# The later modulation vectors of layer 0: two pairs of column blocks gathered in one accumulator bank

## The chip, the cores and the metric

The kernel runs on one core of a Trainium2 chip. The metric is the device time of one execution in microseconds (us); the median of three runs of the kernel before is 1124.67 us.

## What is computed

A two-layer backbone on 512 tokens of width 1024 with a context prefix of 256 tokens. Everything is float32. What matters here is the modulation: six vectors of 1024 values for each layer, made from one conditioning vector c.

```python
def ada_mod(cvec, w, b, dtype):
    m = jax.nn.silu(cvec.astype(jnp.float32)) @ w.astype(jnp.float32) + b.astype(jnp.float32)
    return jnp.split(m.astype(dtype), N_MOD, axis=-1)
...
sh1, sc1, g1, sh2, sc2, g2 = ada_mod(c, w_ada[i], b_ada[i], h.dtype)
n_x = modulate(rms_norm(h, norm_mix_g[i]), sh1, sc1)
...
y_x, _, _ = even_mixer(n_x, ep, s_f, s_b)
h = h + g1[:, None] * y_x
h = h + g2[:, None] * sq_relu_mlp(modulate(rms_norm(h, norm_mlp_g[i]), sh2, sc2), mlp_w1[i], mlp_w2[i])
```

The even mixer of layer 0 joins a bidirectional state-space scan over 32 channel groups with a gated convolution, and ends in an output projection. The change touches the third to fifth vector of layer 0 (g1, sh2, sc2), which are needed only from the output projection on.

## The kernel before, in words

The program is a list of tile operations in `mixer0` and in the stage behind it. A scheduler decides in which order each engine gets them, so a small edit can move many instructions. Each engine runs its own queue strictly in order: TensorE (PE, with its weight loads PEld), VectorE (DVE), ScalarE (ACT), GpSimd (POOL) and the one DMA queue, which SyncE (SP) issues.

**Where the change sits.** In `mixer0` the input projection comes first, then eight steps of the scan (`step_params` prepares a step, `step_main` runs it: `ps_v` on PE, the chain `rr`, `tv`, scan, `ua`, `ub` on DVE, copies `sc` on ACT, `ps_y` on PE). Other work is filled in between the steps by a table of letters: `FILL0` behind the first three `step_params`, `FILL` behind the steps. `v` is a projection of the convolution branch (`ps_vg`, 48 matmuls), `c` a convolution (`ps_cv`), `y` and `z` the outputs of the scan (`ps_t`, `ge`), `k` and `g` the gate (`gw`, `ps_gl`), `h` the load of the residual stream, `n` the norm of the convolution (`ps_mu`, `ps_ms`, `ps_r`), `w` the output projection (`ps_o`), and `a3` means three calls of `ada_rest`.

**The later modulation vectors.** `ada_rest(m, d)` makes 2 x 128 columns of vector m. The 1024 conditioning values lie in `S2` as eight slices of 128 rows, each padded with zeros to 32 columns, so that a slice can be the stationary operand of a quarter of the array. `ada_pe` (L353 to L370) loads two blocks of 128 columns (512 KB each, L223), and for each block issues eight matmuls of 128 columns, four of them side by side in the four column groups (L363). The four partial sums lie in four groups of 32 partitions of the bank `ps_ada`; ACT copies them to `ada` (L139), and one small matmul for each block (L369) with the selector `sel` adds the four and turns the row into a column. DVE adds the bias into `mod` (L113). There are 12 such calls: 24 loads, 192 tile matmuls, 24 small ones, 12 copies and 12 additions. Float32 matmuls leave two records each in the trace.

**What they share.** The loads go through the ring `wraw` of three buffers, which also holds the projection weights (`win_vg`), the weights of the last convolution (`CW`), those of the gate (`wglu`) and of the output projection (`wout`). A load is issued when the buffer's user three allocations earlier is done, and whatever stands behind it on the DMA queue waits too: the shifted copies for the convolution (`cvt<-vpad`), the small transfers of the scan's kernels (`Kt<-sd`, and `hx<-sd` for steps 2 and 5), and the residual stream. `ps_ada` shares a pair of banks (tag "c") with `ps_vg`, `ps_cv` and others.

```python
for i, w in enumerate(ws):
    for kt in (0, 2, 4, 6, 1, 3, 5, 7):
        j = kt // 2
        PE.matmul(ps[32 * j:32 * j + 32, i * 128:i * 128 + 128], S2[:, kt, :], w[kt],
                  start=kt % 2 == 0, stop=kt % 2 == 1, tile_position=(0, 32 * j))
```

Of the kernel before, what the change touches and what calls it, by code (L numbers as in the profile page):

```python
# [8 lines left out]
F32 = mybir.dt.float32  # L9
# [10 lines left out]
KT = 8  # L20
# [25 lines left out]
    g="VVVVVVVVVVVVVVVVVVVVVVVVVVVVVVVVVVVVVVVVVVVVVVVV", e="VVVVVVVVVVVVVVVVVVVVVVVVVVVVVVVVVVVVVVVVVVVVVVVV", o="VVVVVVVVVVVVVVVVVVVVVVVVVVVVVVVVVVVVVVVVVVVVVVVV",  # L46
    ra="VVVVVVVVVVVVVVVV", um="VVVVVVVVVVVVVVVVVVVVVVVVVVVVVVVV", ua="VVVVVVVVVVVVVVVVVVVVVVVVVVVVVVVV",
    wv="VVVVVVVV", ln="VVVV", wo="VVVVVVVVVVVVVVVV",
    w="VVVVVVVV", wdb="VVVVVVVV", wub="VVVVVVVV",
# [5 lines left out]
WT = "cc"  # L55
YB = 1
AT = "c"
WU = "r"
REV = (1,)
CWH = ("h", "h", "h", "wraw")  # L60
# [7 lines left out]
XQ = "P"  # L68
OQ = "P"
FOG = 2  # L70
FILL0 = ("v0 a3", "", "")
FILL = ("v1", "", "c0 v2 a2", "c1 c2 v3", "a3 y", "c3", "h k a4 n", "w7 z", "g w9 w9")
NREST = (1, 1, 1, 1, 2, 2, 2, 2)
NB = 16
LB = 5
# [22 lines left out]
def body(tc, I, out, dbg=None):  # L98
    nc = tc.nc
    V, S, G, PE = nc.vector, nc.scalar, nc.gpsimd, nc.tensor  # L100
# [8 lines left out]
    def mul(e, o, a, b):  # L109
        e.tensor_tensor(o, a, b, op=OP.mult)  # L110

    def add(e, o, a, b):
        e.tensor_tensor(o, a, b, op=OP.add)  # L113
# [23 lines left out]
    def copy(e, o, a):  # L137
        if e is S:
            S.activation(o, a, AF.Copy)  # L139
        else:  # L140
            e.tensor_copy(o, a)
# [10 lines left out]
    with tc.tile_pool(name="persist", bufs=1) as P, tc.tile_pool(name="ps", bufs=1, space=PSUM) as PS:  # L152
# [5 lines left out]
        mod = P.tile([128, 2, 6, KT], F32, name="mod")  # L158

        def smv(n):  # L160
            o, w = SM[n]
            return sm[:, o:o + w]

        bada = smv("bada").rearrange("p (l m) -> p l m", l=2)
# [35 lines left out]
        def bank(nm, tag):  # L200
            return PS.tile([128, 512], F32, name=nm, tag=tag, bufs=dict(s=2, c=2, m=1, n=1)[tag])
# [103 lines left out]
        def mixer0(P0):  # L305
            ring = Ring(P0, RING0)
# [9 lines left out]
            sd = P0.tile([128, GQ, 15 * PH], F32, name="sd")  # L316
            stage = sd[0:PH]
            Dd = sd[32:32 + PH].rearrange("p a b -> p (a b)")[:, 0:NG * PH].rearrange("p (q h) -> p q h", h=PH)
            S2 = P0.tile([128, KT, 32], F32, name="S2")
            sel = P0.tile([128, 32], F32, name="sel")  # L320

            def w4(nm, tag, dt=F32, n=512):
# [13 lines left out]

            G.memset(S2, 0.0)
            cs = P0.tile([128, 2, KT], F32, name="cs")
            cT = smv("c").rearrange("p (v k) -> p v k", v=2)
            S.activation(cs, cT, AF.Sigmoid)  # L340
            mul(V, S2[:, :, 0:2].rearrange("p k v -> p v k"), cT, cs)
            V.tensor_reduce(sel, ident.rearrange("p (j r) -> p r j", j=4), axis=mybir.AxisListType.X, op=OP.add)

            def ada_half(src):
# [9 lines left out]
            def ada_pe(srcs, ld, tag="n"):  # L354
                n = len(srcs)
                ws = [l(src) for l, src in zip(ld, srcs)]

                def go():
                    ps = bank("ps_ada", tag)
                    for i, w in enumerate(ws):  # L360
                        for kt in (0, 2, 4, 6, 1, 3, 5, 7):
                            j = kt // 2
                            PE.matmul(ps[32 * j:32 * j + 32, i * 128:i * 128 + 128], S2[:, kt, :], w[kt],  # L363
                                      start=kt % 2 == 0, stop=kt % 2 == 1, tile_position=(0, 32 * j))
                    a = P0.tile([128, 256], F32, name="ada", tag="ada", bufs=1)[:, :n * 128]
                    copy(S, a, ps[:, 0:n * 128])
                    p2 = ps[:, 256:256 + 2 * n]
                    for i in range(n):
                        PE.matmul(p2[:, 2 * i:2 * i + 2], a[:, i * 128:i * 128 + 128], sel[:, 0:2], start=True, stop=True)  # L369
                    return p2.rearrange("p (m v) -> p m v", v=2)  # L370
                return go
# [45 lines left out]
            def u_load(d):  # L417
                adas[d] = ada_pe([I["wada0"][d, 0], I["wada0"][d, 1]], (ada_half, ada_full))
                wus[d] = w4("wu", WU[d % len(WU)])
                dma(wus[d], I["win_u"][d])  # L420
# [77 lines left out]
            dt_, a2, ea, em = small(), small(2 * NG), small(2 * NG), small(2 * NG)  # L498
# [402 lines left out]
            for i in range(0, NG, 4):  # L901
                ps = bank("ps_u", UT[i // 4])
# [14 lines left out]
            x4 = cvt[:, 0:4 * X4].rearrange("p (c t) -> p c t", c=4)  # L917
            cw = smv("cw").rearrange("p (j x) -> p j x", j=4)

            def ada_rest(m, d):  # L920
                p2 = ada_pe([I["wada0b"][m - 2, d], I["wada0b"][m - 2, d + 1]], (ada_full, ada_full), AT)()
                add(V, mod[:, 0, m, d:d + 2], p2[:, :, 0], bada[:, 0, m * KT + d:m * KT + d + 2])

            rest = [(m, d) for m in (2, 3, 4) for d in range(0, KT, 2)]
            ysbs = []
            cacc = []
            vps = []
# [3 lines left out]
            def fill(what):  # L931
                for x in what.split():
                    if x[0] == "v":
                        vps.append(vgt(int(x[1])))
                    elif x == "z":
                        y_out(1, ysbs[1])
                    elif x == "y":
                        y_out(0, ysbs[0])
                    elif x == "k":
                        glu_load()  # L940
                    elif x == "g":
                        glu_gate()
                    elif x == "n":
                        conv_norm(cacc)
                    elif x == "h":
                        hh.append(htile("h", [128, KT, L]))
                        load_x(hh[0], "xT")
                        for d in range(KT):
                            add_pos(E("hp", d), hh[0], d)
                    elif x[0] == "w":  # L950
                        for _ in range(int(x[1])):
                            p, t, d = oparts.pop(0)
                            out_proj(ring, hh[0], d, (p,), HALF[t], WT)
                    elif x[0] == "c":
                        cacc.append(conv(int(x[1]), vps[int(x[1])]))
                    else:
                        for _ in range(int(x[1])):
                            ada_rest(*rest.pop(0))

            for st in range(3):  # L960
                QS.append(step_params(st))
                fill(FILL0[st])
            for st in range(NST):
# [3 lines left out]
                if st + 3 < NST:  # L967
                    QS.append(step_params(st + 3))
                fill(FILL[st])
            fill(FILL[NST])  # L970
            ts(mod[:, 0, 4], mod[:, 0, 4], 1.0, OP.add)
# [3 lines left out]
        with tc.tile_pool(name="pre", bufs=1) as P0:  # L975
            EPOS = (V, G, V, G, V, G, V, G)
            h, oparts = mixer0(P0)


        with tc.tile_pool(name="main", bufs=1, reuse_waits="tile") as M:  # L980
            crow = M.tile([128, D], F32, name="crow", tag="junk")
            csil = M.tile([128, D], F32, name="csil", tag="csil")
            ring = Ring(M, RING1)


            for t, tk in enumerate(HALF):
                for d in range(KT):
                    ps = tuple(p for p in (1, 0) if (p, t, d) in oparts)
# [87 lines left out]
            for i in range(2):  # L1076
                w = ring.raw(I["pw"][2 * i:2 * i + 2].rearrange("g p m k c -> p g m k c"), [2, 2, 2, 128])
# [67 lines left out]
            for tk in HALF:  # L1145
                n = tk.stop - tk.start
# [43 lines left out]
def layout(inp):  # L1190
    a = {k: np.asarray(v) for k, v in inp.items()}
    X = {}
# [20 lines left out]
    X["sm"] = np.concatenate([parts[n] for n in SM], axis=1)  # L1213
    wa = a["w_ada"].reshape(2, KT, 128, 6, KT, 128)
    X["wada0"] = wa[0][:, :, 0:2].transpose(3, 2, 1, 0, 4)
    X["wada0b"] = wa[0][:, :, 2:5].transpose(2, 3, 1, 0, 4)
    wt = a["w_ada"].transpose(0, 2, 1)
    X["wadaT"] = np.concatenate([wt[0, 5 * D:].reshape(KT, 128, D), wt[1].reshape(6 * KT, 128, D)], axis=0)
    perm = [(2 * bb + gh) * 8 + i for bb in range(2) for i in range(8) for gh in range(2)]
# [49 lines left out]
```

## Time and profile before

| | |
|---|---|
| median of three runs (range) | 1124.67 us (1123.05 to 1126.91) |
| the profiled execution, and its span | 1127.26 us, 1125.1 us |
| PE busy | 1045.0 us, 93% of the span |
| DVE busy | 810.7 us, 72% |
| ACT busy | 514.6 us, 46% |
| mean granted TensorE clock | 0.969 of full |

The profiled execution took 2.2 us more than its span, and 2.6 us more than the median of the runs. Shares over the whole span are averages: the mixer fills the first third, where PE, DVE and the DMA queue wait for each other in turn; the MLPs fill the rest, where PE is nearly always busy. What an edit in the mixer is worth is read from the stretch in which it sits. In the rows below a timeline row gives the start, the time from the first start to the last end of what it merges, the engine, the line and the operation, and in brackets the idle time before it and what ended that. "Granted clock" (PEclk) is TensorE's clock as a share of 2.4 GHz.

### The profile page before, as it was taken

Reading aid. Unit: us, or ns where it says so; the run is one execution under the profiler, and the core shown is the slowest. Engines: PE = TensorE matmul, PEld = TensorE weight load, DVE = VectorE, ACT = ScalarE, POOL = GpSimd, SP = SyncE. Lnnn points to the kernel's source line nnn. Section 1 sums busy time; section 2 is a strip of 40 time slices with the busy share of each in tenths; the row PEclk is TensorE's granted clock in tenths of the full one; section 3 lists DMA queues with packets and bytes.
Section 4 is the critical chain, followed back from the end, with each engine's and each line's share of the span. In section 5 each row is a group of like instructions: output and inputs, shape, how many; then the busy total and the mean of one; then the engine's idle time right before and its main releaser. Section 6 shows DMA issues by size and latency. Waiting matters only on the chain.

```text
span 1125.1 us, 18913 instructions
## 1 busy us (share of the span) xinstructions
PE 1045.0 (93%) x7342; PEld 892.9 (79%) x7342; DVE 810.7 (72%) x1511; ACT 514.6 (46%) x910; POOL 23.8 (2%) x44
## 2 busy tenths in 40 slices
PE   3879998985998999999999999989989999999996
PEld 2657665544788988888789999989989988888896
DVE  7965699778688989868746679899866553343365
ACT  4365544454755643313325456566545332133253
POOL 0002000000000000000000000000000000000000
PEclk9999899997899999999999999999989999999998
DMA  9430634145546788878745555545535522233252
GB/s 348 146 128 30 184 85 148 44 123 187 160 137 208 208 281 290 304 230 282 242 149 170 182 174 186 162 133 177 160 121 181 178 94 94 95 108 97 94 169 94
DMA packets 63594, 185.09 MB, mean 165 GB/s; under 512 B 8464, under 2 KB 14608, under 8 KB 63376
## 3 DMA queue, kind: packets, MB, share of 16 engines
q1 hardware_dynamic: 63504, 183.87, 50.6%
q8 instruction: 58, 0.95, 0.3%
q14 instruction: 32, 0.26, 0.1%
HBM read 175.22 MB, written 2.10 MB: 158 GB/s over the span
## 4 chain that ended last, share of the span: by engine, by line
PE 53%; DMA 8%; DVE 6%; ACT 1%; issue 1%; POOLq 0%; POOL 0%; DVEq 0%; ACTq 0%
PE ps L150 17%; PE ps L149 17%; PE ps L148 17%; DMA wraw<-in_wadaT 5%; DMA wraw<-in_w 3%; DVE junk L1000 2%; DVE wlo L116 2%; ACT whi L139 1%; PE ps_o L148 0%; PE ps_r L194 0%; DVE tn L125 0%; PE ps_o L150 0%; PE ps_o L149 0%; PE ps_p L150 0%; PE ps_p L148 0%
## 5 line engine op out<-in xcount | busy, mean ns | idle before, releaser
L139 ACT ACTIVATE whi<-wraw 128x1024 fp32r<-128x1024 f32 (+1 forms) x232 | 231.7, 1000 | 397.2 <-PE ps L149 268.9
L116 DVE TENSOR_TENSOR wlo<-wraw,whi 128x1024 fp32r<-128x1024 f32 (+1 forms) x232 | 266.3, 1149 | 107.4 <-ACT whi L139 104.5
L148 PE MATMUL ps<-nh,whi 128*128 128x256 f32 (+3 forms) x768 | 245.8, 322 | 4.4 <-ACT nh L285 2.5
L150 PE MATMUL ps<-nh,wlo 128*128 128x256 f32 (+3 forms) x768 | 246.4, 322 | 1.8 <-DVE wlo L116 1.7
L149 PE MATMUL ps<-nl,whi 128*128 128x256 f32 (+3 forms) x768 | 246.7, 322 | 1.2 <-DVE nl L125 1.2
L148 PE MATMUL ps<-hh,whi 128*128 128x512 f32 (+3 forms) x768 | 244.3, 318 | 0.0
L150 PE MATMUL ps<-hh,wlo 128*128 128x512 f32 (+3 forms) x768 | 243.7, 317 | 0.1
L149 PE MATMUL ps<-hl,whi 128*128 128x512 f32 (+3 forms) x768 | 243.4, 317 | 0.0
L148 PEld LDWEIGHTS ps<-nh,whi 128*128 128x128 f32 x768 | 148.0, 194 | 15.7 <-ACT nh L285 3.7
L150 PEld LDWEIGHTS ps<-nh,wlo 128*128 128x128 f32 x768 | 148.0, 193 | 13.2 <-DVE wlo L116 3.1
L149 PEld LDWEIGHTS ps<-nl,whi 128*128 128x128 f32 x768 | 148.1, 193 | 11.8 <-DVE nl L125 1.7
L150 PEld LDWEIGHTS ps<-hh,wlo 128*128 128x128 f32 x768 | 144.2, 188 | 12.0 <-DVE wlo L116 0.9
L149 PEld LDWEIGHTS ps<-hl,whi 128*128 128x128 f32 x768 | 144.3, 188 | 10.6
L148 PEld LDWEIGHTS ps<-hh,whi 128*128 128x128 f32 x768 | 144.5, 188 | 9.9
L125 DVE SCALAR_TENSOR_TENSOR h<-ps,mod,h 128x512 f32<-128x512 f32 (+3 forms) x96 | 54.9, 571 | 85.9 <-PE ps L150 85.9
L1000 DVE SCALAR_TENSOR_TENSOR junk<-wraw,csil 128x1024 f32<-128x1024 f32 x56 | 68.3, 1220 | 19.9 <-DMA wraw<-in_wadaT 19.6
L116 DVE TENSOR_TENSOR hl<-rl,hh 128x256 fp32r<-128x256 f32 (+3 forms) x96 | 48.5, 511 | 4.8 <-ACT hh L139 3.7
L1026 ACT ACTIVATE rl<-ps 128x256 f32<-128x256 f32 (+3 forms) x96 | 41.9, 437 | 5.7 <-PE ps L150 4.6
L148 PE MATMUL ps_o<-nh,whi 128*128 128x256 f32 x128 | 38.2, 299 | 3.6 <-ACT whi L139 3.0
L150 PE MATMUL ps_o<-nh,wlo 128*128 128x256 f32 x128 | 37.2, 295 | 1.8 <-DVE wlo L116 1.8
L149 PE MATMUL ps_o<-nl,whi 128*128 128x256 f32 x128 | 36.8, 288 | 0.1
L363 PE MATMUL ps_ada<-wraw,S 128*32 128x128 f32 x512 | 25.7, 311 | 9.4 <-DMA wraw<-in_wada0b 8.5
(266 smaller groups left out, 1371.1 us busy)
## 6 DMA issues: line engine op xcount, KB each, us to landing
wraw<-in_w SPq DMA_DIRECT2D x192, 512.0 KB, 3.5
wraw<-in_wadaT SPq DMA_DIRECT2D x56, 512.0 KB, 4.6
wraw<-in_wada0b SPq DMA_DIRECT2D x24, 512.0 KB, 4.4
wraw<-in_wout SPq DMA_DIRECT2D x32, 256.0 KB, 2.6
cvt<-vpad SPq DMA_DIRECT2D x64, 67.5 KB, 2.0
wah<-in_wada SPq DMA_DIRECT2D x16, 256.0 KB, 3.8
wraw<-in_wada SPq DMA_DIRECT2D x8, 512.0 KB, 8.1
wraw<-in_win_vg SPq DMA_DIRECT2D x8, 512.0 KB, 4.2
```

Source lines behind the costliest of these rows:

```text
L116: e.tensor_tensor(o, a, b, op=OP.subtract)
L125: V.scalar_tensor_tensor(o, a, s, b, op0=op0, op1=op1)
L139: S.activation(o, a, AF.Copy)
L148: PE.matmul(ps, wh, xh, start=first, stop=False)
L149: PE.matmul(ps, wh, xl, start=False, stop=False)
L150: PE.matmul(ps, wl, xh, start=False, stop=last)
L363: PE.matmul(ps[32 * j:32 * j + 32, i * 128:i * 128 + 128], S2[:, kt, :], w[kt], start=kt % 2 == 0, stop=kt % 2 == 1, tile_position=(0, 32 ...
L1000: V.scalar_tensor_tensor(junk, w, 1.0, csil, op0=OP.mult, op1=OP.mult, accum_out=r)
L1026: S.activation(t, ps, AF.Relu)
```

## The change

Two pairs of column blocks now share one bank and one pass. A call of `ada_rest(m, d0)` makes 4 x 128 columns: four loads of 512 KB, each with 4 of the 8 slices and 256 columns (the array on the host is laid out anew for that), and 16 matmuls of 256 columns. For the second pair the stationary slice starts two columns earlier in `S2`, which has eight columns of zeros in front, so that its sums land two partitions further down in the same bank, and all 16 add into it. Then one copy, two small matmuls with the selector columns 0 and 2, and one addition of 4 columns. There are 6 calls in place of 12, and the table of letters places them anew: four pairs behind the first `step_params` (three before), none behind step 2 (two before), four behind step 4 (three before), four behind step 6 (four before).

```diff
-FILL0 = ("v0 a3", "", "")
-FILL = ("v1", "", "c0 v2 a2", "c1 c2 v3", "a3 y", "c3", "h k a4 n", "w7 z", "g w9 w9")
+FILL0 = ("v0 a2", "", "")
+FILL = ("v1", "", "c0 v2", "c1 c2 v3", "a2 y", "c3", "h k a2 n", "w7 z", "g w9 w9")
...
-            S2 = P0.tile([128, KT, 32], F32, name="S2")
+            S2 = P0.tile([128, KT, 40], F32, name="S2")
...
-            def ada_rest(m, d):
-                p2 = ada_pe([I["wada0b"][m - 2, d], I["wada0b"][m - 2, d + 1]], (ada_full, ada_full), AT)()
-                add(V, mod[:, 0, m, d:d + 2], p2[:, :, 0], bada[:, 0, m * KT + d:m * KT + d + 2])
-
-            rest = [(m, d) for m in (2, 3, 4) for d in range(0, KT, 2)]
+            def ada_rest(m, d0):
+                ps = bank("ps_ada", AT)
+                for p in range(NPR):
+                    for kh in range(2):
+                        w = ring.raw(I["wada0b"][m - 2, d0 // 2 + p, kh], [4, 256])
+                        for j in range(4):
+                            PE.matmul(ps[32 * j:32 * j + 32, 0:256], S2[:, 4 * kh + j, 8 - 2 * p:40 - 2 * p], w[:, j],
+                                      start=p == kh == 0, stop=p == NPR - 1 and kh == 1, tile_position=(0, 32 * j))
+                a = P0.tile([128, 256], F32, name="ada", tag="ada", bufs=1)
+                copy(S, a, ps[:, 0:256])
+                p2 = ps[:, 256:256 + 2 * NPR].rearrange("q (i p) -> q i p", i=2)
+                for i in range(2):
+                    PE.matmul(p2[:, i], a[:, i * 128:i * 128 + 128], sel[:, 0:2 * NPR:2], start=True, stop=True)
+                bd, o = (x.rearrange("q (p i) -> q i p", i=2) for x in (
+                    bada[:, 0, m * KT + d0:m * KT + d0 + 2 * NPR], mod[:, 0, m, d0:d0 + 2 * NPR]))
+                add(V, o, p2, bd)
+
+            rest = [(m, d) for m in (2, 3, 4) for d in range(0, KT, 2 * NPR)]
```

The lines of the changed kernel are one higher up to this point. On every engine the order stands as before up to the first of these matmuls, behind the input projection, and again from the output projection on; between them it moves. Three places show how.

On PE, at the start of the scan. `ps_g` turns the first step's operand, `ps_v` is the first step's product (16 matmuls), `ps_vg` the second projection of the convolution branch. Before:

```order
L363 MATMUL ps_ada<-wraw,S_87 32x128 x6
L634 MATMUL ps_g<-ident,gg 128x128 x4
L363 MATMUL ps_ada<-wraw,S_87 32x128 x8
L634 MATMUL ps_g<-ident,gg 128x128 x4
L690 MATMUL ps_v<-U,GT 64x96
L691 MATMUL ps_v<-U,GT 64x96
L690 MATMUL ps_v<-U,GT 64x96
L691 MATMUL ps_v<-U,GT 64x96
L369 MATMUL ps_ada<-sel,ada 128x2 x2
L148 MATMUL ps_vg<-nh,whi 128x512
L149 MATMUL ps_vg<-nl,whi 128x512
L666 MATMUL ps_k<-O,Bb 16x128 x8
```

and in the changed kernel:

```order
L927 MATMUL ps_ada<-wraw,S_87 32x256 x4
L933 MATMUL ps_ada<-sel,ada 128x2 x2
L635 MATMUL ps_g<-ident,gg 128x128 x4
L927 MATMUL ps_ada<-wraw,S_87 32x256 x4
L635 MATMUL ps_g<-ident,gg 128x128 x4
L691 MATMUL ps_v<-U,GT 64x96
L692 MATMUL ps_v<-U,GT 64x96
L691 MATMUL ps_v<-U,GT 64x96
L692 MATMUL ps_v<-U,GT 64x96
L927 MATMUL ps_ada<-wraw,S_87 32x256 x4
L667 MATMUL ps_k<-O,Bb 16x128 x8
L691 MATMUL ps_v<-U,GT 64x96
```

Before, 12 of the 16 `ps_v` stood behind the first two `ps_vg`. Now they stand ahead of them, behind the seventh load's four matmuls; the eighth load's four follow the last `ps_v`.

On PE, in the middle, behind the third projection of the convolution branch. Before:

```order
L363 MATMUL ps_ada<-wraw,S_87 32x128 x2
L634 MATMUL ps_g<-ident,gg 128x128 x4
L363 MATMUL ps_ada<-wraw,S_87 32x128 x8
L666 MATMUL ps_k<-O,Bb 16x128 x8
L363 MATMUL ps_ada<-wraw,S_87 32x128 x6
L690 MATMUL ps_v<-U,GT 64x96
L691 MATMUL ps_v<-U,GT 64x96
L690 MATMUL ps_v<-U,GT 64x96
```

and in the changed kernel, at the end of the same projection:

```order
L151 MATMUL ps_vg<-nh,wlo 128x512
L725 MATMUL ps_y<-Kt,U 64x128 x2
L725 MATMUL ps_y<-O,sc 64x128
L635 MATMUL ps_g<-ident,gg 128x128 x4
L725 MATMUL ps_y<-O,sc 64x128 x3
L725 MATMUL ps_y<-Kt,U 64x128 x2
L725 MATMUL ps_y<-O,sc 64x128 x4
L789 MATMUL ps_cv<-cvt,hx 32x512 x3
L635 MATMUL ps_g<-ident,gg 128x128 x4
L691 MATMUL ps_v<-U,GT 64x96
L692 MATMUL ps_v<-U,GT 64x96
```

The two calls that stood among this step's `ps_g`, `ps_k` and `ps_v` are gone from here; no `ps_ada` stands on PE between the start of the scan and the fourth projection's end.

On the DMA queue, at the fourth to sixth step. `hx<-sd` are the eight transfers for step 5, the first `Kt<-sd` those for step 6. Before:

```order
L780 DMA cvt<-vpad 32x540 x5
L223 DMA wraw<-in_wada0b 128x1024 x2
L678 DMA hx<-sd 16x4x128 x8
L223 DMA wraw<-in_wada0b 128x1024
L780 DMA cvt<-vpad 32x540 x11
L223 DMA wraw<-in_wglu 128x512 x3
L244 DMA h<-in_xT 128x1024
L678 DMA Kt<-sd 16x4x128 x8
L244 DMA h<-in_xT 128x1024 x3
L223 DMA wraw<-in_wglu 128x512
L223 DMA wraw<-in_wada0b 128x1024 x4
L678 DMA Kt<-sd 16x4x128 x8
```

and in the changed kernel:

```order
L224 DMA wraw<-in_wada0b 128x1024 x3
L781 DMA cvt<-vpad 32x540 x5
L224 DMA wraw<-in_wada0b 128x1024 x2
L781 DMA cvt<-vpad 32x540 x9
L224 DMA wraw<-in_wglu 128x512 x2
L679 DMA hx<-sd 16x4x128 x8
L224 DMA wraw<-in_wglu 128x512
L245 DMA h<-in_xT 128x1024 x4
L224 DMA wraw<-in_wglu 128x512
L224 DMA wraw<-in_wada0b 128x1024
L679 DMA Kt<-sd 16x4x128 x8
L224 DMA wraw<-in_wada0b 128x1024 x3
```

Step 5's transfers have moved back, behind five loads of this kind and two of the gate's. Step 6's stood behind one of the four loads of the residual stream and stand now behind all four, a gate load and one more load of this kind.

## Rows read from the trace of the kernel before

**Rows 1.** The page's first part: busy time, share of the span, instructions.
```profile
PE 1045.0 (93%) x7342; PEld 892.9 (79%) x7342; DVE 810.7 (72%) x1511; ACT 514.6 (46%) x910; POOL 23.8 (2%) x44
```

**Rows 2.** Busy us by stretch: PE, PEld, DVE, ACT, POOL; then PEclk, DMA share, GB/s.
```profile
120.00:150.00 30.00, 29.36 (x272) 19.59 (x276) 26.27 (x41) 15.80 (x36) 0.11 (x1) 0.93 0.50 148
150.00:180.00 30.00, 28.27 (x316) 19.60 (x308) 29.49 (x43) 13.09 (x33) 2.23 (x5) 1.00 0.30 73
180.00:210.00 30.00, 27.80 (x216) 17.04 (x207) 27.90 (x47) 15.78 (x39) 0.38 (x4) 0.94 0.46 134
210.00:240.00 30.00, 27.34 (x352) 15.02 (x351) 20.40 (x30) 15.63 (x41) 2.02 (x2) 1.00 0.35 98
240.00:270.00 30.00, 20.43 (x198) 10.55 (x196) 28.32 (x49) 14.33 (x34) 0.11 (x1) 0.89 0.47 152
270.00:300.00 30.00, 25.76 (x231) 19.14 (x232) 20.63 (x41) 19.94 (x38) 1.01 (x1) 0.77 0.52 166
...
400.00:600.00 200.00, 198.77 (x954) 166.39 (x954) 151.69 (x270) 65.97 (x87) 0.00 (x0) 1.00 0.75 247
```

**Rows 3.** Groups of instructions by line, from 100 to 330 us, of `ada_rest`.
```profile
L363 PE MATMUL ps_ada<-wraw,S 128*32 128x128 f32 x384 | 18.6, 311 | 9.3 <-DMA wraw<-in_wada0b 8.5 <-DVE vpad L110 0.7
...
L369 PE MATMUL ps_ada<-sel,ada 128*128 128x2 f32 x48 | 8.1, 274 | 0.6 <-ACT ada L139 0.6
```

**Rows 4.** The tile ps_ada: duration ns min/median/max; first and last start.
```profile
L139 ACT ACTIVATE ada<-ps_ada x20: 361/383/445, 18.1 to 295.1; 128x256 f32<-128x256 f32 x20
L113 DVE TENSOR_TENSOR mod<-ps_ada,sm x12: 138/160/161, 115.2 to 296.6; 128x2 f32<-128x2 f32 x12
```

**Rows 5.** Timeline of PE, full clock: matmuls of 128 columns, 32 wide.
```profile
171.08 0.64 PE L363 MATMUL ps_ada<-wraw,S 128*32 128x128 f32 x16
171.65 0.65 PE L666 MATMUL ps_k<-O,Bb 64*16 64x128 f32 x16
...
175.09 0.42 PE L363 MATMUL ps_ada<-wraw,S 128*32 128x128 f32 x6 [0.70 <-DVE vpad L110]
```

**Rows 6.** Timeline of PE, full clock: the convolution, 512 columns, 32 wide.
```profile
147.27 4.49 PE L788 MATMUL ps_cv<-cvt,hx 128*32 128x512 f32 x38
151.69 0.66 PE L634 MATMUL ps_g<-ident,gg 128*128 128x128 f32 x4
```

**Rows 7.** Timeline of PE at the start of the scan.
```profile
117.34 0.64 PE L363 MATMUL ps_ada<-wraw,S 128*32 128x128 f32 x4 [1.90 <-DMA wraw<-in_wada0b]
...
120.90 1.08 PE L363 MATMUL ps_ada<-wraw,S 128*32 128x128 f32 x16
...
126.78 0.50 PE L150 MATMUL ps_vg<-nh,wlo 128*128 128x512 f32 x1
```

**Rows 8.** Timeline of the DMA queue there (two windows).
```profile
112.13 0.81 SPq L223 DMA_DIRECT2D wraw<-in_wada0b  x2
...
114.57 0.34 SPq L223 DMA_DIRECT2D wraw<-in_win_vg  x1
```

**Rows 9.** Timeline of DVE there: the first step's first product.
```profile
128.27 0.94 DVE L110 TENSOR_TENSOR rr<-ps_v,E 128x768 f32<-128x768 f32 x1
```

**Rows 10.** Timeline of PE from the fourth to the sixth step.
```profile
235.03 0.44 PE L724 MATMUL ps_y<-hx,U 128*64 128x128 f32 x4
...
238.94 0.65 PE L363 MATMUL ps_ada<-wraw,S 128*32 128x128 f32 x16 [1.28 <-DMA wraw<-in_wada0b]
...
262.74 0.70 PE L724 MATMUL ps_y<-Kt,U 128*64 128x128 f32 x4 [6.40 <-DMA Kt<-sd]
```

**Rows 11.** Timeline of the DMA queue there.
```profile
228.48 5.13 SPq L678 DMA_DIRECT2D hx<-sd  x8
...
255.71 0.33 SPq L244 DMA_DIRECT2D h<-in_xT  x1
256.16 5.13 SPq L678 DMA_DIRECT2D Kt<-sd  x8
```

More of the change, by code (lines that the diff above doesn't have):

```diff
@@ L57 @@
 AT = "c"
+NPR = 2
 WU = "r"
@@ L340, in mixer0 @@
             S.activation(cs, cT, AF.Sigmoid)
-            mul(V, S2[:, :, 0:2].rearrange("p k v -> p v k"), cT, cs)
+            mul(V, S2[:, :, 8:10].rearrange("p k v -> p v k"), cT, cs)
             V.tensor_reduce(sel, ident.rearrange("p (j r) -> p r j", j=4), axis=mybir.AxisListType.X, op=OP.add)
@@ L362, in go @@
                             j = kt // 2
-                            PE.matmul(ps[32 * j:32 * j + 32, i * 128:i * 128 + 128], S2[:, kt, :], w[kt],
+                            PE.matmul(ps[32 * j:32 * j + 32, i * 128:i * 128 + 128], S2[:, kt, 8:40], w[kt],
                                       start=kt % 2 == 0, stop=kt % 2 == 1, tile_position=(0, 32 * j))
@@ L957, in fill @@
                         for _ in range(int(x[1])):
-                            ada_rest(*rest.pop(0))
+                            ada_rest(*rest.pop(0)) if rest else None
             for st in range(3):
@@ L1215, in layout @@
     X["wada0"] = wa[0][:, :, 0:2].transpose(3, 2, 1, 0, 4)
-    X["wada0b"] = wa[0][:, :, 2:5].transpose(2, 3, 1, 0, 4)
+    X["wada0b"] = wa[0][:, :, 2:5].reshape(2, 4, 128, 3, 4, 256).transpose(3, 4, 0, 2, 1, 5)
     wt = a["w_ada"].transpose(0, 2, 1)
```

## The prediction

> **What bounds the kernel now.** The busy times come first [rows 1]: PE works 93% of the span, so the question is where it isn't the last to be waited for. The stretches answer that [rows 2]. In the MLP PE is busy 198.77 of 200 us: what the mixer saves is handed on whole, as the order of every engine from the output projection on is unchanged. In the mixer the bound changes hands. From 120 to 210 us both work nearly always (DVE 26.27, 29.49 and 27.90 of 30, PE 29.36, 28.27 and 27.80). From 210 to 240 PE leads (27.34 against 20.40), from 240 to 270 DVE (28.32 against 20.43). From 270 to 300 neither fills the time, and PE has the lowest granted clock, 0.77, that is part of the stretch at 1.2 GHz. So a saving on PE alone counts in some stretches, and a start that both engines can make earlier counts in all.
>
> The groups [rows 3] say what the twelve calls cost PE: 18.6 us in tile matmuls, 8.1 us in small ones, 8.5 us waiting for their loads. The sequence at the start of the scan [rows 7 to 9] shows the place where such a wait holds up everything: PE stands 1.90 us for the fifth load, reads the sixth at 120.90, continues the projection at 126.78, and DVE takes the first step's product at 128.27.
>
> **The change part by part.** The sum is made on the profiled execution (1127.26 us, 2.6 us above the median); the difference is then put on the median.
>
> *Tile matmuls.* 192 of 128 columns become 96 of 256: 384 records become 192. Two spacings at full clock are in the trace. Sixteen short records go from 171.08 to 171.65, 35.6 ns each [rows 5]; 38 records of 512 columns, just as wide, go from 147.27 to 151.69, 116.3 ns each [rows 6]. A record of 256 columns lies between: 35.6 + (116.3 - 35.6) x 128/384 = 62.5 ns. Then 384 x 35.6 = 13.7 us becomes 192 x 62.5 = 12.0 us: **1.7 us less on PE**. The bounds are the two rows themselves, 192 x 35.6 = 6.8 us (6.9 less) and 192 x 116.3 = 22.3 us (8.6 more); the line between is taken, since columns times width is the same work. Here the Trainium skill (TensorEngine Tiling, section Instruction Overhead) says that each matmul costs some 60 cycles whatever its size. At 2.4 GHz that would be 25 ns for each of the 192 records saved, an estimate of 4.8 us in place of 1.7; the two spacings leave only 35.6 - 128 x 0.210 = 8.7 ns that does not grow with the columns, so the trace doesn't bear the page out.
>
> *Small matmuls.* 48 records, 8.1 us [rows 3], become 24: 4.0 us less on PE. *Copies and additions.* Six copies of 0.383 us go from ACT and six additions of 0.160 us from DVE [rows 4]. ACT is busy 46% of the span [rows 1], so 2.3 us there count nothing; DVE saves 1.0 us.
>
> *The start of the scan.* Two more loads stand here, eight in place of six, each read by 4 matmuls of 256 columns instead of 8 of 128. The first three are there early. Load five was issued at 112.13 and PE stood for it until 117.34 [rows 7, 8]; after that, each freed buffer is refilled. At 114.57 the queue issued a projection load [rows 8]; the seventh load now takes its place, and with the same 5.2 us it is there at 119.8. The twelve `ps_v` behind it are now free of the projection's weights, for which they stood behind two `ps_vg` before. After load seven come its four matmuls (8 x 62.5 ns = 0.5 us), the eight `ps_k` (0.65 us from row to row at full clock [rows 5]) and twelve short `ps_v`, some 1 us: 122 us at full clock, 124 at half. So DVE can take the first product at 122 to 124 in place of 128.27: **4.3 to 6.3 us earlier**, and I take 4.5, because the copies of `ps_k` on ACT come first in DVE's queue. The projection's third matmul comes hardly earlier than 126.78: its load is now issued behind loads seven and eight, and DVE splits it after the first product. I count 1.1 us there, one DVE split, with bounds of a load's 5.2 us later and 2 us earlier.
>
> *The middle.* Two calls leave the stretch around 171 us: four loads' matmuls at 0.57 us, two pairs of small ones at 8.1/24 x 2 = 0.7 us each, and the wait of 0.70 us [rows 3, 5], together 4.4 us of PE. With the 1.1 us PE is then 5.5 us ahead at 223 us, and DVE, which works nearly all the time here, keeps its 4.5. Both can therefore keep a lead of some 4.5 us.
>
> *The fourth to sixth step.* Eight loads in place of six, of which three are read at once as before. Five in place of three are then waited for, at up to 1.28 us each [rows 10], less one pair of small matmuls (three become two): 2 x 1.28 - 0.7 = 1.9 us more on PE. DVE has slack there (20.40 of 30), so PE's lead decides and shrinks to 5.5 - 1.9 = 3.6 us. In the tail four calls become two: two pairs of small matmuls and the shorter tile matmuls (a third of the 1.7 us), 1.4 + 0.6 = 2.0 us less on PE, half of which I count, since DVE is the bound up to 270 us; with its own 1.0 us saved the sum is 3.6 + 1.0 = 4.6 us.
>
> *The queue.* Step 6's transfers stood behind a load of the residual stream and were issued at 256.16 [rows 11]; PE waited 6.40 us for them, until 262.74 [rows 10]. They stay behind it, now behind three loads more, 0.4 us each, while the gate's loads and step 5's output come earlier with the rest. I count nothing for that, with bounds of 6.4 us either way (the wait disappears, or comes twice).
>
> **Sum:** 4.6 us less, rounded to 4.5: 1122.8 us in an execution like the profiled one, and against the median **1120.2 us**.
>
> **The rivals.**
>
> *No change to speak of.* The lead at the start is eaten up before the sixth step, because the scheduler has put other work ahead of the chain: preparations for later steps on DVE, a whole projection on PE ahead of the fourth step's last `ps_v`. For it: both engines are above 26 of 30 us busy from 120 to 210, so there is no idle time in which order could be made good. Against it: they are that full with the two calls that leave. What stays is DVE's 1.0 us and a little of PE's: 1123.2 us.
>
> *Slower.* The eight transfers for step 5 were issued at 228.48, 6.55 us before PE used them at 235.03 [rows 10, 11]. Now they stand behind five loads and two gate loads whose buffers are freed by the last of those matmuls. If the second gate load gets its buffer less than 7 us (5.13 us of issuing, 2 us of way) before PE reaches step 5's output, PE waits, as it waited 6.40 us for step 6's, and the clock falls as it did behind that wait (0.77 from 270 to 300 [rows 2]). With another 6.4 us of waiting and some 2 us at half clock against the 4.5 us won: 1124.67 - 4.5 + 8.4 = 1128.6 us. Against it: the last convolution, some 7 us of PE, now stands between.
>
> *Faster by more.* The reverse in the same place: DVE's preparations come early, step 6's transfers are issued before PE needs them, and the 6.40 us and the half clock behind go too. With the 4.5 us: 1124.67 - 4.5 - 6.4 = 1113.8 us. By the page's overhead of 60 cycles alone it would be 3.1 us less than my forecast, 1117.1 us.
>
> *It doesn't do what it says.* A record of 256 columns could cost twice that of 128 and more; then the tile matmuls save nothing, and the forecast loses 1.7 us at most: 1121.9 us. This lies within the range.
>
> **How the numbers follow.** A measurement of this kernel can tell 0.3%, 3.4 us, from no change: under 1121.3 us is faster, over 1128.0 slower. The forecast has a chance of 0.38, faster by more 0.15, no change 0.28 (with it the page's and the record's variants on either side), slower 0.19. Faster is therefore 0.53, the same 0.28, slower 0.19. The forecast's own range, by its start of 4.3 to 6.3 us and the wait of 1.9 us twice or not at all, is 1117 to 1122. For 8 in 10 the range goes down to 1112, just past the faster case, and up to 1128.5, where the slower case begins.
>
> **What would show it.** Right: DVE's first `rr` from `ps_v` at 122 to 124 us; 192 records of `ps_ada` tile matmuls in about 12 to 15 us and 24 small records in about 4; no `ps_ada` from 130 to 220 us; the output projection some 4 us earlier. Wrong: a first `rr` later than 127; a wait of PE for `hx<-sd`; waits for the loads well above 8.5 us; an output projection that starts where it did, with more idle time of DVE between 130 and 240 us.

## The result, and the profile after

The changed kernel takes 1130.67 us (median of 6 runs, 1127.16 to 1134.06) against 1124.18 of the kernel before: ratio 1.0055, 95% interval 1.0035 to 1.0074. By that ratio it is slower by 6.2 us where 4.5 us less had been forecast, and above the 1128.5 us at which the forecast's range ended. The profiled execution took 1132.22 us, its span is 1130.4, 5.3 us more than that of before.

The page's first part, and the groups of the new units from 100 to 330 us (busy us, mean ns of one, idle time before them), answer to [rows 1, 3]:

```profile
PE 1037.3 (92%) x7126; PEld 881.8 (78%) x7126; DVE 809.7 (72%) x1505; ACT 514.4 (46%) x904; POOL 26.1 (2%) x44
```

```profile
L927 PE MATMUL ps_ada<-wraw,S 128*32 128x256 f32 x192 | 16.9, 438 | 8.5 <-DMA wraw<-in_wada0b 8.5
...
L933 PE MATMUL ps_ada<-sel,ada 128*128 128x2 f32 x24 | 3.9, 267 | 2.5 <-ACT ada L140 2.5
```

PE does 7.7 us less work and the kernel is slower. So the work was saved as forecast (18.6 to 16.9 us, 8.1 to 3.9), and PE's idle time grew by more, from 80.1 to 93.1 us. The stretches [rows 2] show where:

```profile
180.00:210.00 30.00, 25.77 (x211) 15.85 (x207) 21.20 (x37) 12.18 (x34) 0.27 (x3) 0.89 0.25 58
...
240.00:270.00 30.00, 13.97 (x156) 6.65 (x155) 29.54 (x50) 15.27 (x34) 0.11 (x1) 0.77 0.38 120
270.00:300.00 30.00, 22.66 (x150) 14.75 (x150) 16.44 (x33) 18.07 (x37) 1.01 (x1) 0.73 0.56 173
...
400.00:600.00 200.00, 197.50 (x945) 165.01 (x944) 153.79 (x274) 65.30 (x86) 0.00 (x0) 1.00 0.75 252
```

From 180 to 210 DVE, which had worked 27.90 of 30 us, works 21.20. From 240 to 270 it is the other way: DVE works 29.54 and PE 13.97 (20.43 before). The last row, in the MLP, is hardly different.

The chain of the scan can be followed by the eight `rr<-ps_v` on DVE, one for each step, counted here from one. ("Step 2" and the like, in the table of letters and for transfers, count from zero: step 4 makes the fifth `rr`.) Their starts in the two timelines (us):

| step | 1 | 2 | 3 | 4 | 5 | 6 | 7 | 8 |
|---|---|---|---|---|---|---|---|---|
| before | 128.27 | 147.43 | 166.64 | 179.61 | 195.29 | 232.17 | 242.88 | 258.71 |
| after | 123.44 | 142.00 | 162.36 | 179.19 | 217.44 | 225.37 | 244.62 | 265.71 |
| difference | -4.8 | -5.4 | -4.3 | -0.4 | +22.2 | -6.8 | +1.7 | +7.0 |

The start is as forecast. By the fourth step the lead is gone, and the eighth step comes 7.0 us late. What DVE did between these marks stands in its windows from the first to the fourth, sixth and eighth `rr` (busy us of PE, PEld, DVE, ACT, POOL, then PEclk); of before:

```profile
128.27:179.61 51.34, 48.97 (x494) 32.81 (x495) 50.55 (x79) 23.95 (x60) 2.34 (x6) 1.00 0.37 103
179.61:232.17 52.56, 49.90 (x488) 29.05 (x480) 41.19 (x67) 25.94 (x65) 0.61 (x5) 0.97 0.38 112
232.17:258.71 26.54, 21.22 (x252) 10.99 (x252) 24.67 (x40) 15.39 (x35) 1.90 (x3) 1.00 0.37 106
```

and of the changed kernel:

```profile
123.44:179.19 55.75, 53.36 (x490) 33.40 (x491) 54.91 (x79) 28.30 (x63) 5.23 (x8) 1.00 0.40 111
179.19:225.37 46.18, 40.06 (x372) 23.06 (x361) 30.85 (x48) 16.86 (x45) 0.39 (x4) 0.93 0.29 78
225.37:265.71 40.34, 24.85 (x280) 13.11 (x282) 37.91 (x65) 22.25 (x49) 2.13 (x3) 0.80 0.45 131
```

In the first window DVE is full in both, and has 4.4 us more to do: it makes six splits of projection weights (`wlo`, 1.2 us each) where it had made two, two that had stood ahead of the first `rr` and two of the next projection. In the second it does 10.3 us less and stands 15.3 us (11.4 before). In the third it does 13.2 us more, and stands only 2.4 us. So work was put off from the second window, in which DVE waited, to the third, in which the scan hangs on it. The timeline of DVE names the wait of the second window, and what stands ahead of the eighth `rr` in the third:

```profile
216.50 1.10 DVE L111 TENSOR_TENSOR vpad<-ps_vg,sg 128x512 f32<-128x512 f32 x1 [9.28 <-PE ps_vg L151]
217.44 0.95 DVE L111 TENSOR_TENSOR rr<-ps_v,E 128x768 f32<-128x768 f32 x1
...
255.03 1.28 DVE L114 TENSOR_TENSOR h<-h,sm 128x512 f32<-128x512 f32 x2
256.63 1.27 DVE L114 TENSOR_TENSOR h<-h,sm 128x512 f32<-128x512 f32 x2
...
259.04 1.27 DVE L114 TENSOR_TENSOR h<-h,sm 128x512 f32<-128x512 f32 x2
260.24 1.21 DVE L114 TENSOR_TENSOR O<-O,to 128x1024 f32<-128x1024 f32 x1
261.38 1.27 DVE L114 TENSOR_TENSOR h<-h,sm 128x512 f32<-128x512 f32 x2
...
265.71 0.96 DVE L111 TENSOR_TENSOR rr<-ps_v,E 128x768 f32<-128x768 f32 x1 [0.20 <-ACT E L140]
```

The 9.28 us are the fourth projection: PE does the rest of a convolution and of that projection before the last four `ps_v` of the fifth step, and `vpad`, ahead of the fifth `rr` in DVE's queue, waits for it. The eight additions of the position table to the residual stream (5.1 us, needed by the output projection only) now stand ahead of the eighth `rr`; before, they began at 260.79, behind it. PE waits for DVE and then for transfers, and its granted clock falls (0.77 and 0.73 in the last two stretches of the mixer above, where it was 0.89 and 0.77); PE's timeline, to be read beside [rows 10]:

```profile
185.59 0.70 PE L725 MATMUL ps_y<-hx,U 128*64 128x128 f32 x4 [4.23 <-DMA hx<-sd]
...
246.66 0.44 PE L725 MATMUL ps_y<-hx,U 128*64 128x128 f32 x4 [0.40 <-DMA hx<-sd]
...
261.60 1.07 PE L667 MATMUL ps_k<-O,Bb 64*16 64x128 f32 x16 [9.37 <-DVE O L114]
265.32 1.08 PE L667 MATMUL ps_k<-O,Bb 64*16 64x128 f32 x16 [2.65 <-DVE sd L114]
268.84 1.08 PE L927 MATMUL ps_ada<-wraw,S 128*32 128x256 f32 x8 [2.44 <-DMA wraw<-in_wada0b]
272.41 0.69 PE L725 MATMUL ps_y<-Kt,U 128*64 128x128 f32 x4 [2.48 <-DMA Kt<-sd]
```

The first of these rows stands ahead of the late fifth step. PE waits 4.23 us for the transfers `hx` of step 2; before, it had no such wait there. The transfers follow DVE's last work on `sd`, and that comes 4.9 us later than before (178.62 in place of 173.70 us), just ahead of the fourth `rr`. The DMA queue before and after, then DVE after:

```profile
173.98 5.12 SPq L678 DMA_DIRECT2D hx<-sd  x8
```

```profile
178.90 5.13 SPq L679 DMA_DIRECT2D hx<-sd  x8
```

```profile
178.62 0.21 DVE L114 TENSOR_TENSOR sd<-sd 16x64 f32<-16x64 f32 x1
...
196.10 1.22 DVE L111 TENSOR_TENSOR tg<-PG,Bb 128x1024 f32<-128x1024 f32 x1 [3.41 <-PE ps_g L635]
```

Behind this wait PE has half of its clock for 5 us (0.50, the level of 1.2 GHz; before, 1.00 in the same 5 us), and from there on it works without a gap up to the `ps_g` for which DVE stands 3.41 us:

```profile
186.00:191.00 5.00, 5.00 (x30) 2.92 (x26) 4.97 (x10) 3.10 (x9) 0.00 (x0) 0.50 0.44 109
```

### The profile page after: what moved, and what is told of

It is laid out like the page before. It is cut to its first block, busy times and chain, and to the rows that moved or that the text cites. A ratio compares the mean times of both kernels' runs of the same rounds, so it can differ in the third digit from the quotient of the medians.

```text
span 1130.4 us, 18450 instructions
## 1 busy us (share of the span) xinstructions
PE 1037.3 (92%) x7126; PEld 881.8 (78%) x7126; DVE 809.7 (72%) x1505; ACT 514.4 (46%) x904; POOL 26.1 (2%) x44
## 4 chain that ended last, share of the span: by engine, by line
PE 50%; DMA 9%; DVE 6%; issue 1%; ACT 1%; POOLq 0%; POOL 0%; DVEq 0%; ACTq 0%
PE ps L150 16%; PE ps L151 16%; PE ps L149 16%; DMA wraw<-in_wadaT 5%; DMA wraw<-in_w 4%; DVE wlo L117 2%; DVE junk L1014 2%; ACT whi L140 1%; DVE tn L126 1%; PE ps_r L195 0%; PE ps_p L151 0%; PE ps_p L149 0%; PE ps_p L150 0%; DVE hl L117 0%; DVE h L126 0%
## 5 line engine op out<-in xcount | busy, mean ns | idle before, releaser
L1014 DVE SCALAR_TENSOR_TENSOR junk<-wraw,csil 128x1024 f32<-128x1024 f32 x56 | 68.2, 1218 | 18.6 <-DMA wraw<-in_wadaT 18.5
L267 ACT ACTIVATE sq<-h 128x256 f32<-128x256 f32 (+2 forms) x64 | 24.9, 408 | 17.6 <-DVE h L126 16.1
```

The lines of the kernel that those rows point to most:

```text
L267: S.activation(q, h[:, d, tk], AF.Square)
L1014: V.scalar_tensor_tensor(junk, w, 1.0, csil, op0=OP.mult, op1=OP.mult, accum_out=r)
```

## The experiments

Ratios are to the kernel before, run on the same chip, with their 95% intervals. Three theories stood: A, the late fifth step; B, the additions to `h`; C, that the table's places don't matter and the wide units cost the time.

**The fourth projection one place later.**

```diff
-"c1 c2 v3", "a2 y"
+"c1 c2", "v3 a2 y"
```

> The changed kernel with the fourth projection moved one place back in the table, so that the last four ps_v of the fifth step stand ahead of it again. Theory A (the late fifth step: DVE stood 9.28 us for that projection and the fifth rr came at 217.4 in place of 195.3): the fifth rr comes near 200, DVE's 9.28 us go, and most of the loss with them, 1124 to 1126 us. Theory B (the eight additions of the position table to h, 5.1 us of DVE, have come ahead of the eighth step): the fifth rr comes early too, but the eighth rr stays near 265 and the time within 2 us of 1130.7. Theory C (the places of the calls don't matter, the wide units do): 1130.7 within 1.5 us.

Measured: 1129.15 us, ratio 1.0037 (1.0022 to 1.0052).

**The additions to `h` behind the eighth step** (each multiplies the table by a 1.0 that ACT makes from that step's `ua`).

```diff
-add(e, hv, hv, pe.to_broadcast([128, 8, 64]))
+stt(hv, pe.to_broadcast([128, 8, 64]), one, hv, OP.mult, OP.add)
...
-"h k a2 n", "w7 z"
+"h k a2 n", "H w7 z"
```

> The changed kernel with the eight additions to h tied to the eighth step's ua, so that DVE does them behind the scan; everything else on PE and DVE keeps its order up to there. Theory B: the eighth rr comes 4 to 5 us earlier (near 261 in place of 265.7), PE's wait of 9.37 us for O shrinks to about 4, and the time is 1125 to 1127 us. Theory A: the additions filled time in which DVE would have waited, the time stays within 1.5 us of 1130.7.

Measured: 1129.59 us, ratio 1.0045 (1.0025 to 1.0065).

**Both.**

> The changed kernel with both edits: the fourth projection one place later in the table, and the additions to h behind the eighth step. Each alone brought the eighth rr 7.6 and 5.2 us earlier in the profile and the time only 1 to 2 us down. If the two losses are separate: the eighth rr comes 128 to 131 us behind the first, as in the kernel before (130.4), and the time is 1124 to 1127 us. If they are the same idle time, counted twice: the time stays at 1128 to 1130 us.

Measured: 1126.18 us, ratio 1.0023 (1.0003 to 1.0043). The windows from the first to the eighth `rr` of the three, in this order (one fence for each kernel, columns as above):

```profile
120.07:258.14 138.07, 124.76 (x1165) 74.14 (x1165) 121.61 (x185) 70.23 (x168) 10.15 (x15) 0.94 0.39 108
```

```profile
121.80:260.46 138.66, 118.92 (x1136) 69.98 (x1140) 118.95 (x183) 67.88 (x159) 7.47 (x15) 0.93 0.41 114
```

```profile
122.26:257.74 135.48, 121.44 (x1165) 70.96 (x1166) 121.45 (x185) 70.60 (x168) 7.49 (x15) 0.97 0.40 108
```

From the first to the eighth `rr` it was 130.4 us before and 142.3 after (DVE busy 116.4 and 123.7, idle 14.0 and 18.6). One edit takes 4.2 of the 11.8 us away, the other 3.6, both 6.8. So in these executions, one of each kernel, both pieces show in the scan and mostly add up. With the first edit the 9.28 us are gone and the fifth `rr` comes at 204.3 us; with the second PE's wait of 9.37 us for `O` is 5.00. But with both the eighth `rr` still stands 135.5 us behind the first, where 128 to 131 had been expected. PE's wait for step 2's `hx` is there in all three (4.23, 4.24 and 4.23 us), and no run takes it away by itself.

In the whole time neither edit alone can be told from the changed kernel, and each missed the time its theory gave it. Both together lie within the 1124 to 1127 us of two separate losses; they take off 0.32% of the 0.55%, at the edge of what the intervals tell apart. Part of what the scan gained was lost again behind it: from the eighth `rr` to the end the three take 871.4, 868.9 and 868.4 us, the changed kernel 864.7 and the kernel before 866.4. In the second kernel DVE does 4.7 us less in the scan; behind it the additions stand (268.63 us, 5.39 us long) ahead of the convolution's norm, which the output projection needs. Whether that cost time there the trace doesn't show: the output projection begins at 293.6 us, before at 294.8.

```profile
268.63 5.39 DVE L126 SCALAR_TENSOR_TENSOR h<-sm,late,h 128x512 f32<-128x512 f32 x8 [0.17 <-ACT late L721]
274.14 2.48 DVE L117 TENSOR_TENSOR cvt<-cvt,mu 128x512 f32<-128x512 f32 x4
```

**Places against units.** The old units in the new places:

```diff
-FILL0 = ("v0 a3", "", "")
-FILL = ("v1", "", "c0 v2 a2", "c1 c2 v3", "a3 y", "c3", "h k a4 n", "w7 z", "g w9 w9")
+FILL0 = ("v0 a4", "", "")
+FILL = ("v1", "", "c0 v2", "c1 c2 v3", "a4 y", "c3", "h k a4 n", "w7 z", "g w9 w9")
```

> The kernel before with its own twelve calls of 128 columns, put where the changed kernel has them (four, none, four, four calls). If the places make the loss: 1128 to 1132 us, with no ps_ada between the start of the scan and the fourth projection and the fifth rr late. If the wide units make it: 1124.2 within 2 us.

Measured: 1136.07 us, ratio 1.0095, 4 us above what the places' theory gave. Next, units of 256 columns and one pair (twelve of two loads and 8 matmuls), with the table of the kernel before:

```diff
-NPR = 2
+NPR = 1
```

> The changed kernel with one pair per unit (two loads, 8 matmuls of 256 columns, twelve units) in the places of the kernel before (3, 2, 3, 4 calls). If the places make the loss: 1124.2 or up to 2 us less, since the tile matmuls take some 1.7 us less of PE. If the wide matmuls themselves are what costs: 1128 us or more.

Measured: 1121.54 us, ratio 0.9971, 0.7 us below what the places' theory gave. The same units in the changed kernel's places (`a4`, none, `a4`, `a4`):

> The one-pair units of 256 columns in the places of the changed kernel (4, 0, 4, 4), the corner that is missing: old units gave 1.0000 in the old and 1.0095 in the new places, one-pair units 0.9971 in the old. If units and places add up: 1.0066, some 1131 to 1133 us, with the fifth rr 90 us or more behind the first and the eighth 138 us or more. If the places only hurt units of 128 columns or of two pairs: below 1127 us.

Measured: 1135.27 us (1131 to 1133 if units and places add up), with the fifth `rr` 92.9 us and the eighth 139.9 us behind the first. The changed kernel with one unit put back behind step 2:

```diff
-"c0 v2", "c1 c2 v3", "a2 y"
+"c0 v2 a1", "c1 c2 v3", "a1 y"
```

> The changed kernel with one of the two calls of step 4 put back behind step 2 (2, 1, 1, 2 units): the only edit is in the table. The fifth step's ps_v stand ahead of the fourth projection again. If what the change lost is its places, and the wide units themselves gain: the fifth rr comes before 206, the eighth 128 to 132 us behind the first, and the time is 1119 to 1123 us. If the places behind step 2 don't matter: within 2 us of 1130.7.

Measured: 1125.26 us, with the fifth `rr` at 193.1 us and the eighth 132.2 us behind the first; the time missed its range by 2 us. The old units in those places, against the kernel before:

```diff
-"v0 a3" ... "a3 y"
+"v0 a4" ... "a2 y"
```

> The kernel before with one call moved from step 4 to the start (4, 2, 2, 4 old calls): the places of the run with one unit put back behind step 2, but with units of 128 columns. If the wide units gain 0.3 to 0.4% wherever they stand: 1.003 to 1.004 against 1.0001 of that run, 1127 to 1130 us. If moving a call to the start is what costs: 1.006 or more.

Measured: 1130.51 us, ratio 1.0056, between the two. And the kernel before with only the calls behind step 2 moved:

```diff
-"c0 v2 a2", "c1 c2 v3", "a3 y"
+"c0 v2", "c1 c2 v3", "a5 y"
```

> The kernel before with the two calls behind step 2 moved to step 4 and nothing else (3, 0, 5, 4 old calls). Here the scheduler leaves the fifth step's 16 ps_v ahead of the fourth projection. If the loss of the changed places comes through that order: the fifth rr stays before 200 and the time within 2 us of 1125. If it comes from the calls that crowd the stretch behind step 4 (their loads, and PE's waits for them at half clock): 1129 us or more, with the loss behind 220 us.

Measured: 1131.85 us, ratio 1.0069, as the second half had it. Last, units of two pairs in the old places, two units of one pair among them to make the odd numbers (the table has `a2`, `a1`, `a2`, `a2` units; in the second kernel the one-pair unit comes first in its place):

```diff
-rest = [(m, d) for m in (2, 3, 4) for d in range(0, KT, 2 * NPR)]
+rest = [(2, 0, 2), (2, 4, 1), (3, 0, 2), (3, 4, 2), (2, 6, 1), (4, 0, 2), (4, 4, 2)]
```

> Five units of two pairs and two of one pair in exactly the places of the kernel before (3, 2, 3, 4 column pairs of 256). If the forecast failed only in what the new table does to the order, and the two-pair units gain 0.4 to 0.55% where the places are equal (1.0095 to 1.0055 and 1.0056 to 1.0001): 0.994 to 0.998 of the kernel before, 1118 to 1122 us, with the eighth rr 128 to 131 us behind the first. If the units gain only in tables that are bad for other reasons: 0.999 to 1.002.

> The same units and places, with the one-pair unit ahead of the two-pair one at the start and behind step 4. Places and units are the same, so by the theory of places and units the time is that of the run beside it within 2 us; a difference of more than that is what the scheduler's order alone is worth.

Measured: 1127.84 and 1127.40 us, ratios 1.0025 and 1.0013: the units gain nothing here. The second kernel differs from the first in order alone, and by 0.4 us in time. Yet in the profiled executions the fifth `rr` came 66.5 us behind the first in one and 83.7 us in the other, and the eighth 127.8 and 132.7 us. So a distance read in one execution doesn't settle the median.

All ratios, by places (pairs of column blocks at the start, behind steps 2, 4 and 6) and units:

| places | 128 columns | 256, one pair | 256, two pairs |
|---|---|---|---|
| 3, 2, 3, 4 | 1 | 0.9971 (0.9957 to 0.9985) | mixed: 1.0025 (1.0004 to 1.0047); 1.0013 (0.9990 to 1.0035) |
| 4, 2, 2, 4 | 1.0056 (1.0035 to 1.0076) | | 1.0001 (0.9981 to 1.0020) |
| 4, 0, 4, 4 | 1.0095 (1.0075 to 1.0115) | 1.0097 (1.0065 to 1.0130) | 1.0055 (the change) |
| 3, 0, 5, 4 | 1.0069 (1.0044 to 1.0095) | | |

Theory C falls: with the old units the new places cost 0.95%, with one-pair units 1.3%. But that places and units add up falls too. Two pairs gain 0.4 and 0.55% at equal places in two rows and nothing in the first, where the mixed kernels missed their 1118 to 1122 us; one pair gains in the first row and nothing in the third. What is left is the order which the scheduler makes of places and units together. That is argued and not shown: the one pair of kernels that differ in order alone came out the same. The windows from the first to the eighth `rr` of two kernels with the old units, in the new places and with nothing behind step 2 but three at the start:

```profile
124.84:265.41 140.57, 119.59 (x1186) 73.48 (x1184) 122.61 (x184) 66.33 (x158) 5.72 (x15) 0.91 0.38 108
```

```profile
127.23:258.22 130.99, 117.74 (x1229) 70.38 (x1227) 121.65 (x189) 67.03 (x160) 5.42 (x13) 0.96 0.42 119
```

In the new places the old units go the way of the change, 140.6 us, with the fifth `rr` 94.0 us behind the first. With nothing behind step 2 but three at the start the fifth step isn't late (67.8 us) and the eighth `rr` comes when it came before; that kernel loses its 0.69% behind it. Its PE waits, and its windows just ahead of the output projection:

```profile
261.76 1.08 PE L363 MATMUL ps_ada<-wraw,S 128*32 128x128 f32 x16 [6.35 <-DMA wraw<-in_wada0b]
...
295.15 0.80 PE L148 MATMUL ps_o<-nh,whi 128*128 128x256 f32 x2 [4.01 <-ACT nh L139]
```

```profile
285.00:295.00 10.00, 4.29 (x28) 3.07 (x20) 7.12 (x15) 9.99 (x17) 0.00 (x0) 0.76 0.26 80
295.00:305.00 10.00, 9.42 (x32) 7.74 (x33) 5.74 (x10) 4.45 (x9) 0.00 (x0) 0.56 0.00 0
```

and the same stretches before:

```profile
285.00:295.00 10.00, 9.19 (x104) 7.03 (x101) 6.60 (x12) 10.00 (x19) 0.00 (x0) 0.85 0.55 176
295.00:305.00 10.00, 9.22 (x63) 8.18 (x63) 9.47 (x19) 7.74 (x15) 0.00 (x0) 1.00 0.40 117
```

PE works 4.29 us of ten, and gets 0.56 of its clock in the next ten; before, it worked 9.19 of the same ten and had 1.00 in the next. The output projection begins at the same time as before (295.2 and 294.8 us) and ends 6 us later. So the same table entry, nothing behind step 2, loses its time in another place here. (The profiled execution of the old units at 4, 2, 2, 4 was the fastest of its twelve, 1124.14 us against a median of 1130.51, so its trace doesn't show its loss.)

**Towards a better table**, with one-pair units: one unit moved from step 6 to step 2; the old places with the additions to `h` behind the scan (as above); one unit moved from step 4 to step 6.

```diff
-"c0 v2 a2", "c1 c2 v3", "a3 y", "c3", "h k a4 n"
+"c0 v2 a3", "c1 c2 v3", "a3 y", "c3", "h k a3 n"
```

> The one-pair units of 256 columns with one call moved from step 6 to step 2 (3, 3, 3, 3 units in place of 3, 2, 3, 4). If the last calls' loads are what PE waits for at the end of the mixer (4.80 and 1.81 us in the run with 3, 2, 3, 4): 1 to 3 us less than that run's 1121.5. If PE is the bound around step 2: 1 to 3 us more.

> The one-pair units in the old places (1121.5 us) with the additions to h behind the eighth step. There only four of the eight additions stand behind the scan's eighth rr and four more shortly behind it, so little is to be had: if DVE bounds the end of the scan, 0 to 2 us less; if the additions then come late for the output projection, 1 to 4 us more.

```diff
-"c0 v2 a2", "c1 c2 v3", "a3 y", "c3", "h k a4 n"
+"c0 v2 a2", "c1 c2 v3", "a2 y", "c3", "h k a5 n"
```

> The one-pair units with one call moved from step 4 to step 6 (3, 2, 2, 5). If PE's waits for the loads ahead of the last convolution bound the stretch behind step 4: 1 to 3 us less than 1121.5. If the loads at the end of the mixer do (PE waited 4.80 and 1.81 us for them there): 1 to 3 us more.

Measured: 1124.64 us (1.0005, 0.9988 to 1.0023), 1124.57 (0.9993, 0.9967 to 1.0019), 1123.70 (0.9999, 0.9974 to 1.0025): none can be told from the kernel before. By the ratios they are 0.34, 0.22 and 0.28% above the one-pair units in the old places, on the side of the second half of each forecast, but for the last two the intervals overlap with that run's: that the additions to `h` behind the scan lose time here is not shown. The one-pair units in the old places stay the best, 1121.54 us (1116.90 to 1125.21), faster than both kernels by their interval. The window of that run:

```profile
120.27:249.71 129.44, 117.70 (x1153) 72.61 (x1151) 118.16 (x185) 65.72 (x158) 6.42 (x15) 0.99 0.38 106
```

It starts the scan 8.0 us earlier than before in the profiled executions and keeps the distance to the eighth `rr` (129.4 us): DVE does 1.8 us more and stands 2.7 us less. That is what had been forecast for the change. Behind the eighth `rr` it takes 2.6 us more (869.0 against 866.4). (Of the 8.0 us some 3 may be the execution's: in kernels with the changed kernel's order up to there the first `rr` came between 120.1 and 123.4.)

## Why the prediction was wrong

- **The start: right.** First `rr` at 123.44 us (forecast 122 to 124), 4.8 us earlier (120.07 to 122.26 in three more kernels with this order up to there). The projection's third matmul came at 127.05, hardly earlier, as said.
- **The units: right.** 24 records of 256 columns took 1.43 us at full clock, 59.6 ns each against 62.5 forecast, as PE's timeline has it to the next matmul:

```profile
217.68 1.50 PE L927 MATMUL ps_ada<-wraw,S 128*32 128x256 f32 x24
219.11 0.66 PE L635 MATMUL ps_g<-ident,gg 128*128 128x128 f32 x4
```

  The small matmuls fell by 4.2 us (4.0), the tile matmuls by 1.7 us (1.7). The group of tile matmuls took 16.9 us, above the 12 to 15 named as a sign: the forecast priced it at full clock (12.0), as it did the old group (13.7 for a measured 18.6), so only the difference came out right. By the overhead that the Trainium skill (TensorEngine Tiling, section Instruction Overhead) gives for each matmul the latter would have been an estimated 4.8 us; the group's row doesn't agree. The records of this group overlap (one lasts 438 ns in the mean), so it says nothing of what a matmul costs by itself. The waits for the loads stayed at 8.5 us in all, where I had added 1.9.
- **The middle: wrong, and here the forecast failed.** "Both can therefore keep a lead of some 4.5 us" took for granted that DVE does the same work ahead of each step as before. It had to make two splits that had been done ahead of the first `rr`, and was given two of the next projection. That is 4.9 us in a stretch in which DVE stood less than 1 us, and the lead at the fourth step was 0.4.
- **The fourth to sixth step: wrong.** "DVE has slack there (20.40 of 30)": it has, but slack that comes too early is lost. DVE stood 9.28 us for the fourth projection, and 10.3 us of its work fell into the stretch where PE hangs on it, with the 5.1 us of additions. The sum had no term for this; measured, it is 13.2 us of DVE work more between the sixth and the eighth `rr`. (The sum also names two savings of 1.0 us, half of PE's 2.0 and DVE's own, and adds one.)
- **The rivals.** "No change to speak of" named what happened: work on DVE ahead of the chain, and a whole projection on PE ahead of the fifth step's last `ps_v` (the prediction, counting from zero, calls it the fourth). Its price was wrong: I let it eat the lead and stop there. An order that is no longer matched to the waits can cost more than the lead it was given. The slower rival's mechanism, PE waiting for `hx` and then working at half clock, came too, but at step 2 (4.23 us) and by way of DVE's later work on `sd`; at the rival's place, step 5, it cost 0.40 us. DVE was busy during the 4.23 us and stood 3.41 us later on; how much of the loss this wait makes isn't shown. `Kt` of step 6 cost 2.48 us in place of 6.40.
- **Handed on whole.** From the eighth `rr` to the end it took 866.4 us before and 864.7 after, so in this pair the scan's loss did go through, though the output projection, forecast some 4 us earlier, began at 304.2 us in place of 294.8. That a gain goes through whole isn't shown: in the profiled executions of the other kernels this last part took 867.9 to 875.8 us. The clean sum is -4.8 (start) + 11.8 (scan) - 1.7 (behind it) = +5.3 us.

What stays open: of the 0.55%, taking away two named pieces brings back 0.32%. In the profiled execution with both edits the scan is still 5.0 us longer than before and the part behind it 2.0 us longer. Of the scan's rest, PE's wait for step 2's `hx` with the half clock behind it wasn't tried alone, nor were the splits that DVE does earlier; no edit of the table moved them without moving other things.

## What to carry to other kernels

Where a scheduler or planner makes the order, an edit of the work is also an edit of the order, and the second can be the larger one: price it from the new order, engine by engine, up to the next point where an engine is waited for. Count what each engine does between two marks of the chain (here the `rr`) in the old and the new order; a lead is kept only if no engine that is already full between these marks is given more to do. After a change of units, try the table anew, first with the places as they were and the smallest of the new units: here that was the one kernel that gained (0.29%).

## What the runs showed of the hardware

A product on DVE can become much longer beside a POOL instruction. In the run with nothing behind step 2, POOL worked on `CW` for 1.91 us, and the DVE product that started 0.05 us later took 2.41 us; the same product took 0.68 us when POOL was idle:

```profile
231.56 1.91 POOL L110 TENSOR_TENSOR CW<-sm,sel 128x1024 f32<-128x1024 f32 x1 [3.19 <-PE ps_ada L363]
```

```profile
229.48 0.68 DVE L110 TENSOR_TENSOR ge<-ge,yx 128x512 f32<-128x512 f32 x1
...
231.61 2.41 DVE L110 TENSOR_TENSOR ge<-ge,yx 128x512 f32<-128x512 f32 x1
```

Not every product does. In the kernel before, a product that reads `ps_v` from an accumulator bank ran inside the same `CW` at its usual 0.96 us:

```profile
231.94 1.91 POOL L110 TENSOR_TENSOR CW<-sm,sel 128x1024 f32<-128x1024 f32 x1 [29.79 <-PE ps_ada L363]
```

```profile
232.17 0.96 DVE L110 TENSOR_TENSOR rr<-ps_v,E 128x768 f32<-128x768 f32 x1 [2.69 <-PE ps_v L691]
```

In the run with the later projection it was POOL's work that became longer: the same `CW` took 5.43 us, while DVE worked without a gap, and PE waited 2.19 us for it. The spacing of matmul records 32 wide at full clock was 35.6, 59.6 and 116.3 ns for 128, 256 and 512 columns; a line through any two of the three leaves 3 to 12 ns that don't grow with the columns.
